# Third seven-product pair in the first two downs of each feed-forward, with the residual added in HBM

## The chip, the cores and the metric

One core of a Trainium2 chip (trn2) runs the whole block in one launch. The metric is device time in microseconds (us), the median of several executions. The engines are TensorE (PE; its weight loads are the separate row PEld), VectorE (DVE), ScalarE (ACT), GpSimd (POOL) and SyncE (SP), which here only issues DMA transfers.

## The reference

One layer of a streaming encoder on 256 tokens with 2048 features, in float32. Only the two feed-forwards matter here, each with 5632 hidden features:

```python
def swiglu(h, w_gate, w_up, w_down):
    return (jax.nn.silu(h @ w_gate) * (h @ w_up)) @ w_down

x = x + 0.5 * swiglu(rms_norm(x, ffn1_norm[l]), ...)
# pooling and gated linear attention on rms_norm(x), one output projection, added to x
# attention over 256 memory tokens, added to x
x = x + 0.5 * swiglu(rms_norm(x, ffn2_norm[l]), ...)
out = rms_norm(x)
```

## The kernel before

**Precision.** Every float32 operand is split into a high and a low part in fp32r: ScalarE copies the high part (`wh` of a weight, lines 279, 491, 1720), VectorE subtracts it to get the low part (`wl`, lines 280, 455). A product is then three matmuls: high by high, high by low, low by high.

**Units.** A projection is cut into units of one 1 MB weight load: two blocks of 128 rows (a pair) by 1024 columns. A plain unit multiplies both token halves by all four 128x512 blocks with 24 matmuls of 512 columns (`products`, line 362). A seven treats the pair as a 2x2 block matrix and takes 7 block products P1 to P7 in place of 8, 21 matmuls (`seven`, line 509). For that VectorE makes four sums of weight blocks (`T`, line 488), of which high and low parts are taken as well (`th`, `tl`; the plain blocks' parts are `rh`, `rl`, in the tiles xh and xl), and once per pair four sums of the activations (`Sums.make`, lines 426 to 438), whose parts go to the tile ye and back into ys. P1 and P2 need neither sum; P3 and P4 use a sum on one side alone: P3 one of activations, P4 one of weights. P5, P6 and P7 need both.

**A block** (`block_s`) is 8 units over 1024 columns. It accumulates in four PSUM tiles of two banks: two hold the directly usable results (P2 and P4; P3 and P0), two the partial ones (P1 and P6; P7 and P5). Only four such tiles exist. After the block's last seven, `combine` (lines 583 to 588: one ScalarE copy of P1, three VectorE sums) turns the partial ones into an SBUF tile `sg` and frees their PSUM tiles. After the block's last unit the two others are joined with it (`join`, line 598) or, if `merge` is given, the combined part has already been added to the residual (`early_parts`, line 781) and the rest is added straight from PSUM (`residual`, line 769).

**A feed-forward** (`ffn`) runs in three parts of 4, 4 and 3 column blocks of 512 hidden features. Each part has gate and up blocks (all of them with four sevens, `ORDER`), the turning of the hidden features into `ys` (transposes on line 791), and a down: two blocks of 1024 output columns, which the prediction calls the halves A and B. The first two downs of a part of four (`WHOLE`) have 8 units per half, two of them sevens (pairs 0 and 4). The residual lies in HBM, in X[0] and X[1]; in each half of a down it is fetched (`fetch_x`), added to, and stored again (`store_x`). The first down fetches the input instead.

**Order.** A `Stream` lists units and other steps; `st.op(f, n)` puts a step behind the next n units. Weights are split two units ahead (AHEAD) and loaded three (RAW). The low and high parts of weights form one chain on VectorE and one on ScalarE (`in_turn`); `among_weights` puts a step into that chain, so that it comes after the parts emitted so far and before the next ones. Buffers tie the two ends: wh and wl have three buffers each, so a unit's parts wait until the unit three places before it has left TensorE. A step marked as a `clump` tells the unit before it to hand the last 768 of its 2048 low-part columns to GpSimd (`low_parts`, line 459). Within these bounds the order on each engine is fixed when the kernel is built. All loads and stores of X and all weight loads are issued by SP, one after another.

Of the kernel before, what the change touches and what calls it, by code (L numbers as in the profile page):

```python
# [8 lines left out]
F32R = mybir.dt.float32r  # L9
AF = mybir.ActivationFunctionType  # L10
ALU = mybir.AluOpType
# [3 lines left out]
P = 128  # L15
D = 2048
S = 256
# [3 lines left out]
NB = 512  # L21
# [9 lines left out]
G_FFN1, G_MIX, G_X, G_MEM, G_FFN2, G_PS, G_HN, G_BA, G_END = 0, 16, 32, 48, 64, 80, 88, 96, 100  # L31
# [68 lines left out]
def build(ctx, tc, I, out):  # L100
    nc = tc.nc
    st = Stream()
# [7 lines left out]
    scope = {"stack": None}  # L110
# [34 lines left out]
    def uid(s):  # L145
        cnt[0] += 1
        return f"{s}{cnt[0]}"
# [21 lines left out]
    def ctl(name, shape):  # L169
        return whole_lines(const, shape, F32, name, name)  # L170
# [7 lines left out]
    for t in range(PAD):  # L178
        nc.gpsimd.memset(invc[:, t : t + 1], 1.0 / (t + 1))
    gains = ctl("gains", [P, G_END])  # L180
    Rcol = ctl("Rcol", [P, 2])
    Rm = ctl("Rm", [P, 2])
    ss = ctl("ss", [P, 2, 8])
    sums = ctl("sums", [P, 2])
# [85 lines left out]
    def among_weights(f):  # L270


        scalar, vector = behind_weights(f)
        latest["vector"] = vector
        if scalar is not None:
            latest["scalar"] = scalar
# [22 lines left out]
    def finish_norm(n, spread_too=True):  # L299

        nc.vector.tensor_reduce(out=sums, in_=ss[:, :, :n], axis=AX.X, op=ALU.add)
        done = rsqrt(Rcol, sums, D, 2)
        if spread_too:
            diag["R"] = [diagonal(Rcol[:, t : t + 1]) for t in range(2)]
        return done
# [100 lines left out]
    class Sums:  # L406
# [8 lines left out]
        def make(self, g):  # L415
            act, i = self.act, self.pairs.index(g)
            n = 3 if self.over else 4
            if self.own and (i == 0 or i >= self.room):
                room, tag = (self.room, self.name) if i == 0 else (1, f"{self.name}{i}")
                t = scope["pool"].tile([P, room * 6 * P], F32R, tag=tag, name=uid(tag))  # L420
                held = min(len(self.pairs), self.room) if i == 0 else 1
                t = t[:, : held * 2 * n * P].rearrange("p (g a n s) -> p g a n s", a=2, n=n, s=P)
                self.where.update({i + k: t[:, k] for k in range(held)})
            own = self.where[i]
            a, k = jtile(), slice(2 * g, 2 * g + 2)
            nc.vector.tensor_tensor(
                out=a.rearrange("p (k s) -> p k s", k=2), in0=f32(act[:, k, 0, :]),
                in1=f32(act[:, k, 1, :]), op=ALU.add,
            )

            a = a.rearrange("p (n s) -> p n s", n=4)
            p11, p21, p12, p22 = (a[:, m] for m in range(4))
            nc.vector.tensor_tensor(out=p11, in0=p11, in1=p21, op=ALU.subtract)
            nc.vector.tensor_tensor(out=p21, in0=p22, in1=p21, op=ALU.subtract)
            nc.vector.scalar_tensor_tensor(
                out=p22, in0=p11, scalar=-1.0, in1=p22, op0=ALU.mult, op1=ALU.subtract
            )
            added = nc.vector.tensor_tensor(out=p12, in0=p12, in1=p22, op=ALU.add)
            split(own[:, 0], own[:, 1], a[:, 4 - n :])
            if self.over:  # L440
                split(act[:, 2 * g, 0, P:], act[:, 2 * g, 1, P:], p11)
            return None, added
# [370 lines left out]
    class IntoX:  # L813
# [7 lines left out]
        def make_sums(self, after=None):  # L821
            for g, n in zip(self.sums.pairs, after or self.after):
                st.op(lambda g=g: among_weights(lambda: self.sums.make(g)), n)

    WHOLE = IntoX((0, 4), (2, 5), ((1, 2, 3, 5, 0, 6, 4, 7), (1, 2, 0, 3, 4, 5, 6, 7)),
                  ((0, 4), (0, 4)))
    MIXED = IntoX((0, 4), (1, 4), ((1, 2, 3, 6, 0, 5, 4, 7), (1, 2, 3, 0, 4, 5, 6, 7)),
                  ((0, 4), (0, 4)), room=2, folds=(1, 1, 2, 2))
    OUTPUT = IntoX((0, 4, 6), (0, 4, 9), ((1, 2, 3, 5, 0, 6, 4, 7), (1, 2, 0, 3, 4, 5, 6, 7)),
# [4 lines left out]
    def into_x(w, act, scale, gain=None, k0=0, nk=KT, spread_too=True, src=None, way=OUTPUT,  # L834
               spread_at=3, behind=None):

        for b in range(2):
            st.op(lambda b=b: fetch_x(b, src), 2)
            cols = wwide(w, b * 2 * NB, k0, nk)
            if way.sevens[b]:  # L840
                block_s(cols, act, way.sums, way.orders[b], residual(scale, b, 0),
                        early_parts(scale, b), way.sevens[b], behind=None if b else behind)
            else:
                block_t(cols, act, residual(scale, b))
            if gain is not None:
                for j in range(2):
                    st.op(lambda c=2 * b + j: fold(c, gain), way.folds[2 * b + j])
        if gain is not None:
            st.op(lambda: finish_norm(4, spread_too), way.folds[3] + 1)
            if spread_too:  # L850
                st.op(spread_norm, spread_at)

    FF_PARTS = ((0, 4), (4, 4), (8, 3))

# [4 lines left out]
    def ffn(wg, wu, wd, down, amid=None, end=None):  # L859
# [19 lines left out]
        def ev_up(j, c, held=gate):  # L879
            g = held[j]  # L880
            for h in range(2):
                nc.vector.scalar_tensor_tensor(
                    out=g[:, h, :], in0=c[:, h, :], scalar=Rcol[:, h : h + 1], in1=g[:, h, :],
                    op0=ALU.mult, op1=ALU.mult,
                )

# [53 lines left out]
        return nc.scalar.activation(sums, Rcol, AF.Silu), done  # L940

    st.op(lambda: among_weights(first_factor), 6)
    st.op(more_gains, 14)
    st.op(lambda: turn_gains(G_MIX, G_END), 35)

# [5 lines left out]

    def down_first(wd, k0, nk, last, way):
        way.make_sums()
        if last:
            for g, after in zip(qk_sums.pairs[:2], (9, 11)):
                st.op(lambda g=g: among_weights(lambda: qk_sums.make(g)), after)
        into_x(wd, ys, 0.5, G_MIX if last else None, k0, nk, src=None if k0 else I["x"][0],
               way=way, spread_at=7)

    ffn(I["ffn1_w_gate"][0], I["ffn1_w_up"][0], I["ffn1_w_down"][0], down_first,  # L960
        amid_first)
# [309 lines left out]
    def low_rank():  # L1271
# [4 lines left out]
            sevens=(1, 3))  # L1276
# [226 lines left out]
    def down_last(wd, k0, nk, last, way):  # L1503
        if last:
            down_end(wd, k0, nk, way)
        else:
            way.make_sums()
            into_x(wd, ys, 0.5, None, k0, nk, way=way)

    def end_parts(b):  # L1510
        def home():
# [7 lines left out]
    def down_end(wd, k0, nk, way):  # L1519
# [29 lines left out]
        def last_part(i):  # L1549
            return acc_ps[i][:, 0, : NB // 2]  # L1550
# [14 lines left out]
        def update(nb, h):  # L1565
            xn = x_cols(nb * NB, NB)[:, h]
            return nc.vector.scalar_tensor_tensor(
                out=xn, in0=acc_ps[nb][:, h, :], scalar=0.5, in1=xn, op0=ALU.mult, op1=ALU.add
            )

        def square(nb, h):
# [4 lines left out]
        def last_update(i):  # L1576
            xn = x_cols(3 * NB, NB)[:, 1, columns(i)]
            return nc.vector.scalar_tensor_tensor(
                out=xn, in0=last_part(i), scalar=0.5, in1=xn, op0=ALU.mult, op1=ALU.add
            )  # L1580

        def last_square(i):
# [96 lines left out]
        for b in range(2):  # L1679
            into = lambda j, ps: acc_ps.__setitem__(2 + j, ps)  # L1680
            block_s(wwide(wd, b * 2 * NB, k0, nk - 2), ys, way.sums, END_ORDER[b],
                    into if b else residual(0.5, 0, None), early_parts(0.5, b), (0,),
                    home=end_parts(b), more=b == 1)
        for b in range(2):
            st.unit(wwide(wd, b * 2 * NB, k0 + nk - 2, 2)[0], end_unit(b))
# [76 lines left out]
```

## Time and profile before

| what | value |
|---|---|
| median of 3 runs (lowest to highest) | 2071.29 us (2071.0 to 2071.98) |
| span of the profiled execution, first to last instruction | 2069.6 us |
| TensorE busy, instructions | 2059.1 us (99%), 9464 |
| VectorE busy | 1843.7 us (89%) |
| ScalarE busy | 1173.7 us (57%) |
| GpSimd busy | 103.5 us (5%) |
| mean granted TensorE clock | 0.999 of full |
| DMA: read and written in HBM | 417.58 MB, 16.78 MB |

The profiled execution has no time of its own beside its span: the median of the runs, which are timed without the profiler, is 1.7 us above the span. Matmuls are pipelined, one is issued every 0.227 us though each lasts 0.39 us, so busy times of single groups on TensorE overlap and the share of busy time says little; whether it waited is read from its waits. In a row of the profile stand the line, the engine, the operation, what is written <- what is read, the shape and the count; in the groups by line then the busy time, the mean length of one in ns, and the idle time of the engine before them with what ended it. In rows of the timeline, start and length in us come first. In rows of the stages the columns are the stretch and its length, then busy time of PE, PEld, DVE, ACT and POOL with instruction counts, the granted clock, the share and the rate of the DMA engines.

### The profile page before, as it was taken

Reading aid. Unit: us, or ns where it says so; the run is one execution under the profiler, and the core shown is the slowest. Engines: PE = TensorE matmul, PEld = TensorE weight load, DVE = VectorE, ACT = ScalarE, POOL = GpSimd, SP = SyncE. Lnnn points to the kernel's source line nnn. Section 1 sums busy time; section 2 is a strip of 40 time slices with the busy share of each in tenths; the row PEclk is TensorE's granted clock in tenths of the full one; section 3 lists DMA queues with packets and bytes.
Section 4 is the critical chain, followed back from the end, with each engine's and each line's share of the span. In section 5 each row is a group of like instructions: output and inputs, shape, how many; then the busy total and the mean of one; then the engine's idle time right before and its main releaser. Section 6 shows DMA issues by size and latency. Waiting matters only on the chain.

```text
span 2069.6 us, 24068 instructions
## 1 busy us (share of the span) xinstructions
PE 2059.1 (99%) x9464; PEld 1714.5 (83%) x9464; DVE 1843.7 (89%) x1720; ACT 1173.7 (57%) x1196; POOL 103.5 (5%) x93
## 2 busy tenths in 40 slices
PE   9999999999999999999999999999999999999998
PEld 7888888888888888888888888888888888888886
DVE  7998899989998779989889787989988999889987
ACT  7654455554554666665765544656554565545554
POOL 0000000000000000000000000000000010000001
PEclk9999999999999999999999999999999999999999
DMA  7666766566666655467655455666577765676664
GB/s 265 205 202 224 243 214 215 184 227 238 225 202 224 226 184 183 163 205 280 225 185 192 159 178 183 203 224 224 171 235 225 239 208 185 225 241 224 210 224 156
DMA packets 123129, 435.92 MB, mean 211 GB/s; under 512 B 9860, under 2 KB 13544, under 8 KB 122632
## 3 DMA queue, kind: packets, MB, share of 16 engines
q1 hardware_dynamic: 122840, 434.12, 62.9%
q8 instruction: 74, 1.21, 0.2%
q14 instruction: 39, 0.32, 0.0%
q10 hardware_dynamic: 176, 0.27, 0.0%
HBM read 417.58 MB, written 16.78 MB: 210 GB/s over the span
## 4 chain that ended last, share of the span: by engine, by line
PE 99%; DMA 0%; DVE 0%; SPq 0%; ACT 0%; POOL 0%; POOLq 0%; issue 0%; DVEq 0%
PE pt L362 64%; PE pt L509 30%; PE ph L791 2%; PE pl L1416 1%; PE pv L1453 1%; PE px L802 1%; PE pp L1049 0%; DMA x<-in_x 0%; PE pa L1077 0%; PE tm L1362 0%; PE po L1215 0%; PE px L728 0%; PE pq L1202 0%; PE pe L362 0%; PE pz L1093 0%; PE po L1218 0%
## 5 line engine op out<-in xcount | busy, mean ns | idle before, releaser
L362 PE MATMUL pt<-wh,xs 128*128 128x512 f32 x2432 | 780.8, 391 | 0.0
L1720 ACT CAST wh<-raw 128x2048 fp32r<-128x2048 f32 x242 | 461.7, 1912 | 228.9 <-PE pt L362 128.0
L455 DVE TENSOR_TENSOR wl<-raw,wh 128x2048 fp32r<-128x2048 f32 (+1 forms) x242 | 515.9, 2140 | 83.9 <-ACT wh L1720 83.7
L362 PEld LDWEIGHTS pt<-wh,xs 128*128 128x128 f32 x2432 | 455.9, 188 | 94.1 <-issue 0.5
L491 ACT CAST wh<-T 128x1024 fp32r<-128x1024 f32 x264 | 277.0, 1054 | 379.0 <-DVE T L488 362.4
L362 PE MATMUL pt<-wl,xs 128*128 128x512 f32 x1216 | 474.0, 390 | 0.0
L362 PE MATMUL pt<-wh,ys 128*128 128x512 f32 x1452 | 458.1, 389 | 0.0
L362 PEld LDWEIGHTS pt<-wh,ys 128*128 128x128 f32 x1452 | 272.5, 188 | 56.1
L455 DVE TENSOR_TENSOR wl<-T,wh 128x2048 fp32r<-128x2048 f32 (+1 forms) x132 | 296.7, 2248 | 5.6 <-ACT wh L491 5.2
L362 PE MATMUL pt<-wl,ys 128*128 128x512 f32 x726 | 283.0, 390 | 0.0
L362 PEld LDWEIGHTS pt<-wl,xs 128*128 128x128 f32 x1216 | 228.4, 188 | 46.2
L280 DVE TENSOR_TENSOR xl<-raw,xh 128x1536 fp32r<-128x1536 f32 x132 | 231.1, 1751 | 10.8 <-ACT xh L279 10.7
L279 ACT CAST xh<-raw 128x1536 fp32r<-128x1536 f32 x132 | 195.5, 1481 | 52.1 <-PE pt L509 30.7
L488 DVE TENSOR_TENSOR T<-T,raw 128x512 f32<-128x512 f32 x264 | 182.0, 690 | 6.8
L488 DVE TENSOR_TENSOR T<-raw 128x1024 f32<-128x1024 f32 x132 | 160.7, 1218 | 0.6
L362 PEld LDWEIGHTS pt<-wl,ys 128*128 128x128 f32 x726 | 136.3, 188 | 28.1
L509 PE MATMUL pt<-xh,xs 128*128 128x512 f32 x416 | 154.9, 389 | 0.0
L509 PE MATMUL pt<-wh,xs 128*128 128x512 f32 x396 | 153.9, 389 | 0.0
L459 POOL TENSOR_TENSOR wl<-raw,wh 128x768 fp32r<-128x768 f32 x44 | 81.6, 1854 | 1389.6 <-DVE wl L455 1366.8
L509 PE MATMUL pt<-wh,xe 128*128 128x512 f32 x320 | 124.3, 389 | 0.0
L509 PEld LDWEIGHTS pt<-xh,xs 128*128 128x128 f32 x416 | 78.1, 188 | 16.2
L509 PEld LDWEIGHTS pt<-wh,xs 128*128 128x128 f32 x396 | 74.3, 188 | 15.4
(274 smaller groups left out, 2081.4 us busy)
## 6 DMA issues: line engine op xcount, KB each, us to landing
raw<-in_ffn_w_down SPq DMA_DIRECT2D x88, 1024.0 KB, 5.5
raw<-in_ffn_w_up SPq DMA_DIRECT2D x80, 1024.0 KB, 5.0
raw<-in_ffn_w_gate SPq DMA_DIRECT2D x77, 1024.0 KB, 5.1
raw<-in_w_in SPq DMA_DIRECT2D x32, 1024.0 KB, 5.0
raw<-in_xattn_w_kv SPq DMA_DIRECT2D x32, 1024.0 KB, 5.0
raw<-in_w_out SPq DMA_DIRECT2D x16, 1024.0 KB, 6.7
raw<-in_xattn_w_q SPq DMA_DIRECT2D x16, 1024.0 KB, 6.2
raw<-in_xattn_w_o SPq DMA_DIRECT2D x16, 1024.0 KB, 5.7
```

Source lines behind the costliest of these rows:

```text
L279: in_turn("scalar", lambda: nc.scalar.copy(hi, src))
L280: in_turn("vector", lambda: nc.vector.tensor_tensor(out=lo, in0=src, in1=f32(hi), op=ALU.subtract))
L362: latest["product"] = nc.tensor.matmul(ps, a, w, start=first and i == 0, stop=last and i == 2)
L455: in_turn("vector", lambda: nc.vector.tensor_tensor(out=lo[:, :n], in0=src[:, :n], in1=f32(hi[:, :n]), op=ALU.subtract))
L459: rest = nc.gpsimd.tensor_tensor(out=lo[:, n:], in0=src[:, n:], in1=f32(hi[:, n:]), op=ALU.subtract)
L488: in_turn("vector", lambda: nc.vector.tensor_tensor(out=o, in0=a, in1=b, op=ALU.add))
L491: in_turn("scalar", lambda: nc.scalar.copy(th[:, c], t[:, c]))
L509: nc.tensor.matmul(banks[n], x, w, start=n in fresh and j == 0, stop=n in ends and j == 2)
L791: rows["turned"] = nc.tensor.transpose(v[:, i, h * P : (h + 1) * P], g[:, h, i * P : (i + 1) * P], ident)
L802: nc.tensor.transpose(v[:, j, h * P : (h + 1) * P], x[:, h, j * P : (j + 1) * P], ident)
L1416: nc.tensor.matmul(ps[:, t, :M], ys[:, 4 * h + d, a, tok], xa["K", h][:, d, b, :], start=i == 0, stop=i == 11,)
L1720: in_turn("scalar", lambda: nc.scalar.copy(hi, raw))
```

## The change

In the first two downs of both feed-forwards the residual no longer passes through SBUF. Each block joins its results in the tile `sg`, and a DMA issued by GpSimd adds that tile to X in HBM (`accum_op=ALU.add`), one transfer of 512 KB per 512 columns. For that X must hold the input from the start: SP copies the input to X inside HBM in 8 transfers of 256 KB, between the 15th and 29th unit of the first feed-forward. The factor 0.5 of the feed-forward moves to the up projection's row factor (`Rup`, one VectorE instruction per norm), and the last downs use 1.0. In the downs that now add in HBM, pair 2 becomes a third seven in each half, the order of the units changes, and the third pair's sums get a tile of the tag `sg`. Combine and joins stand in the chain of weight parts and are clumps there, as in gate and up blocks.

```diff
-    Rcol = ctl("Rcol", [P, 2])
+    factors = ctl("Rcol", [P, 4])
+    Rcol, Rup = factors[:, :2], factors[:, 2:]
...
-        done = rsqrt(Rcol, sums, D, 2)
+        rsqrt(Rcol, sums, D, 2)
+        done = nc.vector.tensor_scalar_mul(Rup, Rcol, 0.5)
...
-                room, tag = (self.room, self.name) if i == 0 else (1, f"{self.name}{i}")
-                t = scope["pool"].tile([P, room * 6 * P], F32R, tag=tag, name=uid(tag))
+                if i == 0:
+                    t = scope["pool"].tile([P, self.room * 6 * P], F32R, tag=self.name, name=uid(self.name))
+                else:
+                    t = scope["pool"].tile([P, 4 * NB], F32R, tag="sg", name=uid("sx"), bufs=2)
...
-    WHOLE = IntoX((0, 4), (2, 5), ((1, 2, 3, 5, 0, 6, 4, 7), (1, 2, 0, 3, 4, 5, 6, 7)),
-                  ((0, 4), (0, 4)))
+    WHOLE = IntoX((0, 4, 2), (2, 5, 4), ((1, 3, 5, 0, 6, 2, 4, 7), (1, 0, 3, 2, 5, 4, 6, 7)),
+                  ((0, 2, 4), (0, 2, 4)))
...
+    def copy_x(i):
+
+        b, rows_i = i % 2, slice(i // 2 * S // 4, (i // 2 + 1) * S // 4)
+        nc.sync.dma_start(X[b][rows_i, :], I["x"][0][rows_i, b * 2 * NB : (b + 1) * 2 * NB])
+
+    def added_to_x(b):
+
+        def evict(j, e):
+            nc.gpsimd.dma_start(
+                X[b][:, j * NB : (j + 1) * NB].rearrange("(h p) n -> p h n", p=P), e,
+                accum_op=ALU.add,
+            )
+        return evict
+
+    def onto_x(w, act, k0, nk, way):
+
+        for b in range(2):
+            block_s(wwide(w, b * 2 * NB, k0, nk), act, way.sums, way.orders[b], added_to_x(b),
+                    sevens=way.sevens[b])
...
-                    out=g[:, h, :], in0=c[:, h, :], scalar=Rcol[:, h : h + 1], in1=g[:, h, :],
+                    out=g[:, h, :], in0=c[:, h, :], scalar=Rup[:, h : h + 1], in1=g[:, h, :],
...
+    for i in range(8):
+        st.op(lambda i=i: copy_x(i), 15 + 2 * i)
...
     def down_first(wd, k0, nk, last, way):
         way.make_sums()
-        if last:
-            for g, after in zip(qk_sums.pairs[:2], (9, 11)):
-                st.op(lambda g=g: among_weights(lambda: qk_sums.make(g)), after)
-        into_x(wd, ys, 0.5, G_MIX if last else None, k0, nk, src=None if k0 else I["x"][0],
-               way=way, spread_at=7)
+        if not last:
+            onto_x(wd, ys, k0, nk, way)
+            return
+        for g, after in zip(qk_sums.pairs[:2], (9, 11)):
+            st.op(lambda g=g: among_weights(lambda: qk_sums.make(g)), after)
+        into_x(wd, ys, 1.0, G_MIX, k0, nk, way=way, spread_at=7)
...
-            into_x(wd, ys, 0.5, None, k0, nk, way=way)
+            onto_x(wd, ys, k0, nk, way)
```

The remaining lines put 1.0 for 0.5 where the last down of the second feed-forward is added (`update`, `last_update`, `residual`, `early_parts`).

More of the change, by code (lines that the diff above doesn't have):

```diff
@@ L1567, in update @@
             return nc.vector.scalar_tensor_tensor(
-                out=xn, in0=acc_ps[nb][:, h, :], scalar=0.5, in1=xn, op0=ALU.mult, op1=ALU.add
+                out=xn, in0=acc_ps[nb][:, h, :], scalar=1.0, in1=xn, op0=ALU.mult, op1=ALU.add
             )
@@ L1578, in last_update @@
             return nc.vector.scalar_tensor_tensor(
-                out=xn, in0=last_part(i), scalar=0.5, in1=xn, op0=ALU.mult, op1=ALU.add
+                out=xn, in0=last_part(i), scalar=1.0, in1=xn, op0=ALU.mult, op1=ALU.add
             )
@@ L1681, in down_end @@
             block_s(wwide(wd, b * 2 * NB, k0, nk - 2), ys, way.sums, END_ORDER[b],
-                    into if b else residual(0.5, 0, None), early_parts(0.5, b), (0,),
+                    into if b else residual(1.0, 0, None), early_parts(1.0, b), (0,),
                     home=end_parts(b), more=b == 1)
```

## The prediction

> **What bounds the kernel now.** I read the page first, then TensorE's own waits, then the first down stage engine by engine.
>
> ```profile
> span 2069.6 us, 24068 instructions
> PE 2059.1 (99%) x9464; PEld 1714.5 (83%) x9464; DVE 1843.7 (89%) x1720; ACT 1173.7 (57%) x1196; POOL 103.5 (5%) x93
> ```
> ```profile
> PE pwarm L206 <- POOL ident masks.py:199: 1.4, 1, 1.4
> PE px L728 <- DMA x<-in_x: 0.5, 1, 0.5
> ```
>
> The last two lines are the whole answer on TensorE's waits, and both are at the start. From then on it issues one product after another; VectorE at 89% is the next tightest. So a product removed is worth its full issue time, and that holds only until VectorE is late for the first time. Next, the turning of ys, a seven and a plain unit on PE (chain of the first down: start, length, products), and the first down's two column halves, A and B, in the stage table:
>
> ```profile
> 185.99 1.75 PE ph L791 x16
> ...
> 201.94 4.76 PE pt L509 x21
> 206.70 5.44 PE pt L362 x24
> ```
> ```profile
> 178.00:224.00 46.00, 46.00 (x214) 38.27 (x213) 39.04 (x41) 23.90 (x20) 0.24 (x1) 1.00 0.58 206
> 224.00:265.00 41.00, 41.00 (x182) 33.96 (x181) 39.74 (x31) 20.41 (x15) 0.00 (x0) 1.00 0.76 256
> ```
>
> 5.44/24 = 0.227 us per product, 4.76 us per seven. Columns three to five of the stage rows are PE, weight load and VectorE: VectorE works 39.0 of 46 us in A and 39.7 of 41 in B (the granted clock is 1.00). The question is whether the VectorE work of another seven fits, and at the right moment.
>
> **The change part by part.**
>
> *Products.* 4 downs x 2 halves x 1 more seven x 3 products x 0.227 us = 5.44 us less PE work (1.36 per down). That is all there is to win: 0.26%.
>
> *What VectorE loses and gains.* Rows of A's first down, from the VectorE timeline (start, length):
>
> ```profile
> 171.73 1.23 DVE L585 TENSOR_TENSOR sg<-pt,sg 128x1024 f32<-128x1024 f32 x1
> ...
> 182.10 2.28 DVE L455 TENSOR_TENSOR wl<-raw,wh 128x2048 fp32r<-128x2048 f32 x1
> 185.74 2.29 DVE L455 TENSOR_TENSOR wl<-raw,wh 128x2048 fp32r<-128x2048 f32 x1 [1.35 <-ACT wh L1720]
> ...
> 201.10 1.22 DVE L488 TENSOR_TENSOR T<-raw 128x1024 f32<-128x1024 f32 x1
> ...
> 205.36 2.28 DVE L455 TENSOR_TENSOR wl<-T,wh 128x2048 fp32r<-128x2048 f32 x1
> 207.56 0.68 DVE L426 TENSOR_TENSOR j<-ys 128x512 f32<-128x512 f32 x1
> ...
> 209.47 0.29 DVE L438 TENSOR_TENSOR j<-j 128x128 f32<-128x128 f32 x1
> 209.68 2.28 DVE L455 TENSOR_TENSOR wl<-raw,wh 128x2048 fp32r<-128x2048 f32 x1
> 211.88 0.55 DVE L286 TENSOR_TENSOR ye<-j,ye 128x384 fp32r<-128x384 f32 x1
> ...
> 219.60 0.69 DVE L584 TENSOR_TENSOR sg<-pt,sg 128x512 f32<-128x512 f32 x1 [3.14 <-ACT sg L583]
> ```
>
> and, from the groups by line (count, busy, mean ns of one, idle time before):
>
> ```profile
> L781 DVE SCALAR_TENSOR_TENSOR x<-sg,x 128x1024 f32<-128x1024 f32 x26 | 31.4, 1216 | 0.0
> ...
> L583 ACT COPY sg<-pt 128x512 f32<-128x512 f32 x39 | 22.8, 586 | 57.8 <-PE pt L509 56.7 <-issue 1.1
> ...
> L459 POOL TENSOR_TENSOR wl<-T,wh 128x768 fp32r<-128x768 f32 x6 | 11.2, 1863 | 393.8 <-DVE wl L455 393.8
> ```
>
> Costs go from start to start, since instructions overlap a little: a plain unit's low part 2.2 (209.68 to 211.88), a seven 6.46 (201.10 to 207.56; its low part alone 2.2), the sums of ys for one pair 2.1 (207.56 to 209.68) plus about 0.5 for the low part of ye, and anything of 128x1024, as L781, a join or the low part of a turned block, 1.15 (its 1.22 less the same overlap). Per half the change adds 6.46 - 2.2 = 4.3 for the seven and half a set of sums, 1.3. It removes two of L781, 2.3 (L769 turns into a join of the same size), and, because combine and joins now stand as clumps, two low parts hand 768 of 2048 columns to GpSimd (L459, 1.86 there), 768/2048 of 2.2, 0.8 each: 1.6. Net +1.7 per half, while PE's time falls by 0.7. On average that still fits A; what matters is when it comes.
>
> *The order in A, step by step.* Let T=0 be the down's first product (178.12). The new order is plain 1, plain 3, plain 5, seven 0, plain 6, seven 2, seven 4, plain 7; the three sums are due after units 2, 4 and 5. VectorE is through with unit three's low part at 184.3, T=6.2, as now, and from there its order is forced:
> seven 0 +6.46 = 12.7; turned low parts 2.3 and sums 0 2.1: 17.1; plain 6: 19.3; seven 2: 25.8; sums 2, 2.6: 28.4; seven 4: 34.8; sums 4: 36.9 (their high part, a ScalarE copy under L583's 0.59, by 37.4); plain 7's low part: 39.1; low part of sums 4: 39.6.
> The same list for the kernel before (plain 5, sums 0, turns, seven 0, plain 6, seven 4) ends seven 4 at 207.56, T=29.4: its present 1.35 us of idle time goes, and 6.9 us are added (4.3 + 2.6).
> PE needs: four plain units 21.8, two sevens 9.5 and 16 transposes 1.8 take it to T=33.1. Of seven 4, three products (P1, P2, P4: 9 matmuls, 2.0 us) need no sums, but P4 needs the low part of 34.8, so PE is done with them at about 35.2. Then it can issue plain 7's first product in each of its four banks (0.9) and P7's two high ones (0.45), and waits for the high part of the sums at 37.4: 0.9 idle. Six products follow to 38.8, then it waits again for 39.1 to 39.6: 0.3 to 0.8. That is 1.2 to 1.7 with full filling. What it can't avoid even if every filler is placed well: 0.9. If nothing is filled in, it stands from 35.2 to 39.1: 3.9. TensorE's order is fixed when the kernel is built. Today's shows filling, not always the best:
>
> ```profile
> 214.18 0.23 PE pt L362
> 214.40 1.36 PE pt L509 x6
> 215.76 2.49 PE pt L362 x11
> 218.26 1.36 PE pt L509 x6
> ```
>
> In the same chain, where seven 4 ends today, products of the last plain unit (L362) stand among the seven's (L509). So I take 1.8 per down, nearer the filled end. Below zero it cannot go: there is no TensorE wait left to recover.
>
> *The next places.* After A, low part of B's first unit 1.4 (T=41.0), combine after seven 4's last product (about 40.9, then ScalarE's 0.6 and 0.69 + 1.2 + 0.69): 44.1; B's second unit is now seven 0, 5.6 with its shared low part: 49.7; the two joins 2.3: 52.0. PE gets to that seven at 43.3 + 1.8 + 5.4 = 50.5, and 9 of its products go into banks that the joins don't hold: 52.5. It fits by 0.5. Behind it the sevens of B alternate with plain units (4.76 + 5.44 on PE against 6.46 + 2.2), and VectorE regains its lead. B thus keeps its 0.68.
>
> *Transfers.*
>
> ```profile
> X<-x SPq DMA_DIRECT2D x28, 512.0 KB, 6.9
> x<-X SPq DMA_DIRECT2D x28, 512.0 KB, 4.2
> ...
> x<-in_x SPq DMA_DIRECT2D x8, 256.0 KB, 7.7
> ```
> ```profile
> ACT wh L1720 <- DMA raw<-in_ffn_w_down: 11.3, 7, 2.9
> ```
>
> SP loses 16 stores and 16 fetches. A store waits on SP for the residual, and weight loads queue behind it: ScalarE's 11.3 us of waiting for down weights. TensorE waited for none of it: worth nothing. SP gains 8 copies of 256 KB inside HBM, ahead of weight loads in the first feed-forward; the nearest row lands in 7.7 us, the weights are asked for three units (15 us) ahead: nothing, or if uncovered one late load of the present size, 2.9 us at most. The 16 adding transfers have no row. By the nearest (6.9 us for 512 KB) and even at five times that, 35 us, the next writer of their tile is the combine of the next gate block, seven units (some 36 us) on, and the next reader of X is a whole feed-forward part away. They stand behind VectorE's joins on GpSimd's queue, where the next instruction is a shared low part some 20 us later. Nothing, then; 0 to 2 us if the queue costs something at the start or end. The extra two-column multiplication at four norms is under the 0.29 us of a 128x128 sum (L438) each, and no PE wait stands there now: nothing, 1.2 at most.
>
> *Sum.* 4 x (1.8 - 1.36) = +1.8 us on the span of 2069.6; the median of the runs, 2071.29, lies 1.7 above that span and I keep that distance: 2073.1. Unknown ends per down: 0.9 and 3.9 idle give -1.8 and +10.2 us in all.
>
> **The rivals.**
>
> *Faster: the third seven is absorbed.* If PE's fixed order fills the hole or VectorE gets there 1.5 us earlier than I count, idle time is at most 0.3 per down: 2071.3 - 4.2 = 2067.1, at best 2065.9. For it: no PE wait at all today, and that seven 4's low part today comes 4.3 us before its unit starts (T=29.4 against 33.8, which is five plain units, a seven and the transposes). Against it: its low part comes 5.4 us later, and PE needs it 0.7 earlier.
>
> *Slower: B's second unit waits for A's joins.* Today combine starts at T=41.5, since 11 products of the plain unit are issued ahead of the seven's last six. If that is kept behind plain 7's low part, they end at 39.1 + 17 x 0.227 = 43.0, combine at 46.2, the joins at 54.1, 1.6 after the 52.5 where PE runs out: 1.8 + 1.6 idle per down, 4 x (3.4 - 1.36) = +8.2: 2079.5. It decides from seven 4's last product later than T=41.4 on (40.9 and the 0.5 to spare).
>
> *Slower: GpSimd's pieces hold VectorE up.* The change adds four pieces of a low part per down.
>
> ```profile
> 171.23 1.86 POOL L459 TENSOR_TENSOR wl<-raw,wh 128x768 fp32r<-128x768 f32 x1 [44.03 <-DVE wl L455]
> ```
>
> The combine's sum that starts within this one, at 171.73, reads PSUM and takes 1.23, as long as one of its size with no piece beside it (201.10: 1.22). If a piece came to lie beside a seven's sums and those had to wait for it, one per down at B's second unit would cost 1.86 - 0.5 = 1.4: 4 x 1.4 on top of the forecast, 2078.7. Against it: the pieces stay tied to units ahead of combine and joins. [...]
>
> **How the numbers follow.** This kernel's measurement can tell about 0.2% (4.1 us) from no change. Forecast (0.9 to 2.3 idle per down: -1.8 to +3.8) 0.46, with its own range 2069.5 to 2075.1; absorbed 0.22; joins late (or nothing filled in at A's pair of sevens, the 3.9) 0.27; pieces in the way 0.05. So faster 0.22, same 0.46, slower 0.32. The range reaches from the middle of the absorbed case, 2067, to the slower one's, 2080.
>
> **What the profile after would show.** Products: 9440 instead of 9464 on PE. L781 at 10 instead of 26, 16 more GpSimd-issued transfers, X<-x at 12 on SP. Right: in each first-half A a PE gap of 1 to 2 us at the second of two sevens in a row, VectorE without idle time for the 33 us before, and B without a gap. Wrong if PE shows no such gap (then VectorE's chain is shorter than 39 us or PE had more to fill in), if the gaps are at B's second unit, or if TensorE waits for weights or for X.

## The result: 2099.69 us, slower by 1.35%

| kernel | median of its runs | ratio to before, 95% interval |
|---|---|---|
| before | 2071.49 us | 1 |
| after | 2099.69 us (2095.7 to 2103.02) | 1.0135 [1.0123, 1.0147] |

The profiled execution took 2103.02 us (span 2101.2); it is the longest of the four runs. Every number of the trace of after is to be held against that span: +31.6 us on the span of before. The page of after, span and busy times:

```profile
span 2101.2 us, 24114 instructions
...
PE 2069.2 (98%) x9440; PEld 1713.6 (82%) x9440; DVE 1860.3 (89%) x1768; ACT 1188.6 (57%) x1220; POOL 150.9 (7%) x124
```

The products went as planned (9440 instructions), VectorE has only 17 us more to do in all, and yet TensorE's busy time rose by 10 us with fewer products in it. Its waits (releaser, us in total, times, longest):

```profile
PE pt L513 <- ACT ye L286: 11.3, 4, 3.5
PE pt L513 <- ACT xh L280: 2.6, 2, 1.5
PE pt L513 <- DVE wl L459: 2.5, 4, 0.6
PE pt L364 <- DVE wl L459: 1.6, 1, 1.6
...
PE pt L513 <- DVE sg L602: 1.2, 4, 0.3
PE pt L513 <- ACT ys L286: 1.2, 4, 0.3
```

Lines are shifted by a few (362 is 364, 509 is 513, 455 is 459, 285/286 is 286/287). The first line is new and the largest: in each of the four downs one seven stands for 2.4 to 3.5 us, and not for VectorE but for ScalarE, which makes the high part of the sums (`ye`). The fourth line is a single wait at the start. The first down, timeline of ScalarE, then SyncE's queue, TensorE and VectorE (start, length; in brackets the idle time before and what ended it):

```profile
216.12 3.70 ACT L1747 CAST wh<-raw 128x2048 fp32r<-128x2048 f32 x2
219.96 0.30 ACT L286 CAST ys<-j 128x128 fp32r<-128x128 f32 x1
221.76 1.47 ACT L280 CAST xh<-raw 128x1536 fp32r<-128x1536 f32 x1 [1.50 <-DMA raw<-in_ffn_w_down]
223.14 0.51 ACT L286 CAST ye<-j 128x384 fp32r<-128x384 f32 x1
...
216.86 6.88 SPq L642 DMA_DIRECT2D raw<-in_ffn_w_down  x2
...
219.06 0.50 PE L513 MATMUL pt<-wl,ys 128*128 128x512 f32 x1 [0.63 <-DVE wl L459]
...
220.31 0.50 PE L513 MATMUL pt<-wh,ys 128*128 128x512 f32 x1 [0.29 <-ACT ys L286]
...
223.70 0.80 PE L513 MATMUL pt<-xh,ye 128*128 128x512 f32 x1 [2.42 <-ACT ye L286]
224.29 0.63 PE L513 MATMUL pt<-xl,ye 128*128 128x512 f32 x1
...
215.04 1.75 DVE L281 TENSOR_TENSOR xl<-raw,xh 128x1536 fp32r<-128x1536 f32 x1
216.71 2.29 DVE L459 TENSOR_TENSOR wl<-T,wh 128x2048 fp32r<-128x2048 f32 x1
218.92 0.68 DVE L430 TENSOR_TENSOR j<-ys 128x512 f32<-128x512 f32 x1
...
220.82 0.29 DVE L442 TENSOR_TENSOR j<-j 128x128 f32<-128x128 f32 x1
```

Read it backwards. TensorE stands until 223.70 for `ye`. ScalarE began that copy at 223.14, although VectorE had had the sums ready at 221.11 (last of L442). In between ScalarE copied `xh`, the direct blocks of a seven's weights, and before that it had stood idle for 1.50 us for their transfer. That seven is B's second unit. Its transfer was issued at 216.86, just after VectorE's L281 of seven 4 had ended (216.79) and given the raw buffer back.

The second thing in those rows is the length of the matmuls after the wait: 0.63 and 0.43 from one start to the next, where 0.39 and 0.227 were usual. Stages around that wait and around the one at the start (columns as in the stage rows of before; the column after the five engines is the granted clock):

```profile
220.30:223.70 3.40, 0.97 (x3) 0.49 (x4) 3.37 (x5) 1.88 (x2) 0.00 (x0) 0.97 0.24 98
223.70:227.10 3.40, 3.40 (x8) 2.74 (x9) 1.49 (x2) 0.00 (x0) 2.02 (x1) 0.52 0.77 240
227.10:230.50 3.40, 3.40 (x16) 2.81 (x15) 0.00 (x0) 0.44 (x1) 0.00 (x0) 1.00 0.90 296
...
35.80:39.20 3.40, 3.40 (x10) 2.63 (x9) 2.75 (x5) 2.63 (x4) 0.00 (x0) 0.50 1.02 418
```

After the wait TensorE was granted half its clock for 3.4 us: 8 matmuls where 3.4/0.227 = 15 fit. There are five such stretches (at 35.8, 223.5, 479.5, 1592.3 and, twice as long, 1848.3), 20.4 us together. For 2.3 us of them TensorE was still waiting, and each matmul in the rest takes 0.427 in place of 0.227 us; counted so, the half clock cost 8.5 us, 7.1 of it in the downs. These stretches are "busy" time in the page, which is the largest part of why TensorE's busy time rose. The kernel before has none until its last matmul.

Where the 31.6 us went, counted on TensorE as start-to-start time above 0.227 us, in the steps longer than 0.33 us: 30.5 in the four downs (6.3, 6.2, 9.0 and 9.0), 4.6 more than before in the first 50 us (1.5 of it the clock), -5.4 for the products; about 2 us are spread over the rest and not assigned. The 30.5 are 18.8 us of waits, 7.1 of half clock and 4.6 that the steps beside the waits take longer.

### The profile page after: what moved, and what is told of

The parts are those of the page before. It is cut to its first block, busy times and chain, and to the rows that moved or that the text cites. A ratio compares the mean times of both kernels' runs of the same rounds, so it can differ in the third digit from the quotient of the medians.

```text
span 2101.2 us, 24114 instructions
## 1 busy us (share of the span) xinstructions
PE 2069.2 (98%) x9440; PEld 1713.6 (82%) x9440; DVE 1860.3 (89%) x1768; ACT 1188.6 (57%) x1220; POOL 150.9 (7%) x124
## 4 chain that ended last, share of the span: by engine, by line
PE 92%; DVE 3%; DMA 3%; ACT 1%; issue 0%; SPq 0%; POOL 0%; POOLq 0%; DVEq 0%; ACTq 0%
PE pt L364 57%; PE pt L513 30%; DMA raw<-in_ffn_w_down 2%; PE ph L795 1%; DVE T L492 1%; DMA raw<-in_ffn_w_gate 1%; ACT xh L280 1%; DVE wl L459 1%; PE pl L1443 1%; PE pv L1480 1%; DVE xl L281 1%; PE px L806 0%; DMA x<-in_x 0%; DVE sg L602 0%; PE pp L1076 0%
## 5 line engine op out<-in xcount | busy, mean ns | idle before, releaser
L1747 ACT CAST wh<-raw 128x2048 fp32r<-128x2048 f32 x234 | 445.8, 1912 | 199.8 <-PE pt L364 104.5
L459 DVE TENSOR_TENSOR wl<-raw,wh 128x2048 fp32r<-128x2048 f32 (+1 forms) x234 | 487.8, 2095 | 71.5 <-ACT wh L1747 71.3
L495 ACT CAST wh<-T 128x1024 fp32r<-128x1024 f32 x280 | 294.0, 1054 | 384.3 <-DVE T L492 373.5
L364 PE MATMUL pt<-wh,ys 128*128 128x512 f32 x1324 | 422.2, 391 | 0.0
L459 DVE TENSOR_TENSOR wl<-T,wh 128x2048 fp32r<-128x2048 f32 (+1 forms) x140 | 312.7, 2233 | 6.9 <-ACT wh L495 6.5
L364 PEld LDWEIGHTS pt<-wh,ys 128*128 128x128 f32 x1324 | 249.9, 189 | 51.9
L364 PE MATMUL pt<-wl,ys 128*128 128x512 f32 x662 | 259.5, 392 | 0.0
L280 ACT CAST xh<-raw 128x1536 fp32r<-128x1536 f32 x140 | 207.3, 1480 | 88.3 <-PE pt L513 39.5
L281 DVE TENSOR_TENSOR xl<-raw,xh 128x1536 fp32r<-128x1536 f32 x140 | 245.2, 1751 | 10.8 <-ACT xh L280 10.7
L463 POOL TENSOR_TENSOR wl<-raw,wh 128x768 fp32r<-128x768 f32 x56 | 104.4, 1864 | 1410.8 <-DVE wl L459 1388.0
```

The lines of the kernel that those rows point to most:

```text
L280: in_turn("scalar", lambda: nc.scalar.copy(hi, src))
L281: in_turn("vector", lambda: nc.vector.tensor_tensor(out=lo, in0=src, in1=f32(hi), op=ALU.subtract))
L364: latest["product"] = nc.tensor.matmul(ps, a, w, start=first and i == 0, stop=last and i == 2)
L459: in_turn("vector", lambda: nc.vector.tensor_tensor(out=lo[:, :n], in0=src[:, :n], in1=f32(hi[:, :n]), op=ALU.subtract))
L463: rest = nc.gpsimd.tensor_tensor(out=lo[:, n:], in0=src[:, n:], in1=f32(hi[:, n:]), op=ALU.subtract)
L495: in_turn("scalar", lambda: nc.scalar.copy(th[:, c], t[:, c]))
```

## The experiments

All are set against the kernel before, which ran beside them on the same chips (its medians 2071.47 to 2071.71 us). "Held" means that the copies of the input to X are tied to the weight load before them.

| experiment | median, us | ratio, 95% interval |
|---|---|---|
| e1, copies held | 2098.81 | 1.0133 [1.0116, 1.015] |
| e11, the kernel before with the copies alone | 2074.49 | 1.0013 [1.0004, 1.0022] |
| e7, two sevens, held | 2072.92 | 1.0007 [0.9998, 1.0017] |
| e3, ScalarE's copy of the sums first | 2092.0 | 1.0097 [1.0082, 1.0112] |
| e6, sevens of A spread, held | 2101.25 | 1.0143 [1.0128, 1.0158] |
| e9, third seven in A alone, held | 2080.18 | 1.0038 [1.0025, 1.0052] |
| e8, third seven in B alone, held | 2075.32 | 1.0015 [1.0007, 1.0024] |
| e10, pieces to GpSimd around the sums, held | 2091.13 | 1.009 [1.0076, 1.0104] |
| e12, both, B's second unit plain, held | 2077.21 | 1.0028 [1.0016, 1.004] |
| e13, third seven in B alone, second unit plain, held | 2070.29 | 0.9993 [0.9984, 1.0002] |

**The copies: e1 and e11.** In after, the eight copies were not spread over units 15 to 29: SyncE issued them all between 21.3 and 28.2 us, amid the first weight loads.

```profile
21.27 1.24 SPq L860 DMA_DIRECT2D X<-in_x  x2
22.61 0.53 SPq L642 DMA_DIRECT2D raw<-in_ffn_w_gate  x1
23.18 3.12 SPq L860 DMA_DIRECT2D X<-in_x  x4
26.40 0.54 SPq L642 DMA_DIRECT2D raw<-in_ffn_w_gate  x1
26.98 1.19 SPq L860 DMA_DIRECT2D X<-in_x  x2
...
30.40 1.91 ACT L1747 CAST wh<-raw 128x2048 fp32r<-128x2048 f32 x1 [3.03 <-DMA raw<-in_ffn_w_gate]
```

ScalarE stood 3.0 us for its weights, VectorE 4.4 us for ScalarE's high part, TensorE 1.6 us for the low part (fourth line of the waits). e1 holds the copies:

```diff
-        nc.sync.dma_start(
+        latest["load"] = nc.sync.dma_start(
...
-        nc.sync.dma_start(X[b][rows_i, :], I["x"][0][rows_i, b * 2 * NB : (b + 1) * 2 * NB])
+        with tc.issue_after(latest["load"].ins):
+            nc.sync.dma_start(X[b][rows_i, :], I["x"][0][rows_i, b * 2 * NB : (b + 1) * 2 * NB])
```

> The changed kernel with one edit: each of the 8 copies of the input to X is queued on SP behind the latest weight load, so none can be issued in the first 30 us. Theory (copies drawn forward to 21 to 28 us delay two weight loads, TensorE waits 1.6 us and then runs 3.4 us at half clock): the 4.9 us lost in the first 50 us come back, 2099.7 becomes about 2095, the granted clock shows no half-rate stretch at 36 us, and the four downs are as they were. Rival (the start is lost to GpSimd's queue or to chance): 2099.7 and the gap at 33 us stays.

2098.81 us. In its profile the wait and the half clock at the start are gone, the downs are as in after (`ye` 10.7 us in 4 waits, clock halved behind them). The medians differ by only 0.9 us and their runs overlap (2097.99 to 2100.69 against 2095.7 to 2103.02), so the start's 4.6 us are seen in one profile and not in the times. What is sure is that the downs hold nearly all of the loss. e11 hoists only the copies into the kernel before:

```diff
+    def copy_x(i):
...
+    for i in range(8):
+        st.op(lambda i=i: copy_x(i), 15 + 2 * i)
```

> The kernel before with the 8 copies of the input to X added where the change has them, and nothing else; X is overwritten later as before, so they are idle transfers. Theory (drawn forward to some 21 to 28 us, they delay two weight loads): TensorE waits about 1.6 us near 32 us and the time rises by 1.5 to 5 us, 2073 to 2076.5, the more when the clock halves behind the wait. Rival (that wait came from elsewhere): 2071.5.

2074.49 us, +2.8 (interval 0.8 to 4.6). Its profile shows ScalarE's casts waiting up to 1.4 us for weights near 30 us, but no wait of TensorE there; what stands out on TensorE is a wait of 2.2 us for the input at the very start, with 3.4 us of half clock right behind it. That start wait varies from profile to profile (none in the waits of e7 and e10, 2.2 us here), so how the 2.8 us arise is not settled. That the copies, issued there, cost something is.

**The adds: e7.** Everything of the change but the third seven, with the old orders:

```diff
-    WHOLE = IntoX((0, 4, 2), (2, 5, 4), ((1, 3, 5, 0, 6, 2, 4, 7), (1, 0, 3, 2, 5, 4, 6, 7)),
-                  ((0, 2, 4), (0, 2, 4)))
+    WHOLE = IntoX((0, 4), (2, 5), ((1, 2, 3, 5, 0, 6, 4, 7), (1, 2, 0, 3, 4, 5, 6, 7)),
+                  ((0, 4), (0, 4)))
```

> The changed kernel with two edits: the copies held back as in the run with that edit alone, and the first two downs with two sevens per half in the order of before. What stays of the change: the sums added to X by GpSimd-issued transfers, joins and combine as clumps, the factor 0.5 in the up projection. Theory (the adding transfers cost nothing by themselves; all of the loss is the third seven and the copies): 2071.5, within 2 us of before, and no TensorE wait after the start. Rival (the adding transfers or their issue on GpSimd take from weight loads or from VectorE): 2076 or more, with TensorE waits in the downs or behind them.

2072.92 us, +1.4 with an interval that takes in zero. TensorE waits for nothing in the downs that use the adds. Sixteen GpSimd-issued transfers that add in HBM, clumps, row factor and held copies together cost 3.5 us at most, by the interval: nearly all of the loss comes with the third seven.

**Does moving ScalarE's copy cure it? e3.** The sums are made to return the high part's copy, so that ScalarE's later casts come behind it (in the first two downs of each feed-forward alone; copies not held):

```diff
-            split(own[:, 0], own[:, 1], a[:, 4 - n :])
+            high, _ = split(own[:, 0], own[:, 1], a[:, 4 - n :])
...
-            return None, added
+            return high if self.pairs == (0, 4, 2) and self.act is ys else None, added
```

> The changed kernel with one edit: in the downs that add in HBM, ScalarE's high part of the sums (ye, sx) is put into the chain of weight parts, so that the next weights' high parts come after it. Theory (TensorE waits at the pair of sevens because ScalarE stands before that cast, waiting for a weight load that VectorE's lateness delayed, and the long wait then halves the clock): the four waits for ye of 2.4 to 3.5 us become under 1 us, the low parts of the sums become the next wait, about 1 us, the half-clock stretches in the downs go, and the time falls by 8 to 14 us to 2086 to 2092. Rival (TensorE has to wait for VectorE's chain anyway, ScalarE's order only names the last of several late parts): the wait moves to the low part, the time falls by less than 3 us, and the clock still halves.

2092.0 us. The `ye` wait falls from 11.3 to 1.7 us, and others come, since all casts of weights are now behind the copy:

```profile
PE pt L364 <- DVE wl L459: 7.0, 5, 1.6
PE pt L513 <- DVE xl L281: 4.7, 4, 1.2
PE pt L513 <- DVE wl L459: 3.1, 4, 0.8
PE pt L513 <- ACT ys L286: 2.1, 4, 0.5
PE pt L513 <- ACT ye L286: 1.7, 4, 0.4
```

They add up to 17.0 us in the downs (1.6 of the first row is at the start), nearly as much as in after (18.8), but none is longer than 1.6 us, and nowhere in the profiled run is the clock halved before the last matmul (mean 0.999, after 0.994). Start to start the downs lose 22.5 us, 8.0 less than in after, about the clock's share there (7.1). So in the profiles part of the loss is the clock's. The medians don't price it: three other runs of e3 were granted 0.997, 0.997 and 0.998 and took no longer (2091.74, 2092.26 and 2090.68 against 2092.27).

Nor is it a cure to put ScalarE's copy ahead of all casts. VectorE's last sums now end 39.2 us from the first down's start, where in after they ended at 37.6, since the casts that its low parts need come later: VectorE began one at 200.61 behind 1.7 us of idle time that ScalarE's cast (L1747) ended. Plain 7's cast belongs before the copy, B's second unit behind it; that is the order of e9 and e12 below.

**Is it the pair of sevens at A's end? e6.** Held, copy first as in e3, and A ordered like B, so that no two sevens stand together:

```diff
+    WHOLE = IntoX((0, 4, 2), (0, 4, 2), ((1, 0, 3, 2, 5, 4, 6, 7), (1, 0, 3, 2, 5, 4, 6, 7)),
                  ((0, 2, 4), (0, 2, 4)))
```

> The changed kernel with three edits: copies held back, the sums' high part first on ScalarE, and in half A the order of half B, 1 0 3 2 5 4 6 7, in which the three sevens alternate with plain units (sums due after 0, 4 and 2 units). Theory (the loss in A is three sevens and two sets of sums in a row that VectorE cannot work off in time; alternating them leaves it 6.5 + 2.2 us of work for 10.2 us of products): TensorE waits under 0.5 us per down, no half clock, and the 5.4 us of products are won in part: 2066 to 2070. Rival (VectorE's work per down is too much in any order, or seven 0 in second place is late itself behind the up block): waits of 1 to 3 us per down move to the front of A, 2072 to 2085.

2101.25 us, the slowest of all, with the clock whole (0.999). The waits start right behind the turning of ys and run through A: low parts 7.1 us in 8, `ys` 6.4 in 4, `ys` from ScalarE 4.2 in 8. I read this as VectorE entering a down without a lead, so that the plain units belong at A's front, as the change has them; no run tests that by itself.

**Which half? e9 and e8.** e9 keeps A of the change and gives B its old order with two sevens; its pair 2 in B is a plain unit that multiplies activations which the sums have partly overwritten (same work, other values). e8 has A as before and the three sevens in B, with pair 2's sums due within B. The lines of the change, then those of e9, then those of e8:

```diff
-    WHOLE = IntoX((0, 4, 2), (2, 5, 4), ((1, 3, 5, 0, 6, 2, 4, 7), (1, 0, 3, 2, 5, 4, 6, 7)),
-                  ((0, 2, 4), (0, 2, 4)))
...
+    WHOLE = IntoX((0, 4, 2), (2, 5, 4), ((1, 3, 5, 0, 6, 2, 4, 7), (1, 2, 0, 3, 4, 5, 6, 7)),
+                  ((0, 2, 4), (0, 4)))
...
+    WHOLE = IntoX((0, 4, 2), (2, 5, 9), ((1, 2, 3, 5, 0, 6, 4, 7), (1, 0, 3, 2, 5, 4, 6, 7)),
+                  ((0, 4), (0, 2, 4)))
```

> The changed kernel with the copies held back and the third seven in half A alone: A as in the change, B with the order and the two sevens of before. 12 products less than before, 2.7 us. Theory (A carries the loss): the waits for the sums' high parts stay at 2.3 to 3.5 us per down with half-clock stretches behind them, 2094 to 2099, near the change with held copies (2098.8). Rival (A and B share it: B's late joins and ScalarE's early place for B's second unit, a seven whose weights land late, make A's wait): with a plain unit in B's second place ScalarE has no seven's copy ahead of the sums' part, the waits shrink to the VectorE chain's 1 to 2 us without half clock, 2076 to 2084.

> The changed kernel with the copies held back and the third seven in half B alone: half A has the order and the two sevens of before, half B those of the change, the sums of pair 2 are due after 9 units, in B. 12 products less than before, 2.7 us. Theory (the loss in the downs comes from A's chain; B with its alternating sevens has room): no TensorE wait over 0.3 us in the downs, 2072.9 (two sevens in both halves) less 2.7 is 2070.2, under before by about 1.3. Rival (a third seven is too much for VectorE in either half, or seven 0 in B's second place waits for the joins): waits of 0.5 to 2 us per down at B's second or sixth unit, 2073 to 2080.

e9: 2080.18 us. A is the same as in after, and yet its `ye` wait is 0.4 us per down, not 2.8:

```profile
PE pt L513 <- DVE wl L459: 2.8, 5, 0.6
PE pt L513 <- ACT ye L286: 1.7, 4, 0.4
...
PE pt L513 <- ACT ys L286: 1.2, 4, 0.3
```

So how long A waits is decided by what stands in B. e8: 2075.32 us, 2.4 above e7 with 2.7 us of products less; TensorE waits 1.8 us (4 times 0.5) for `xl` of B's second unit, and its profile has a wait of 1.8 us for the input at the start. Over e7 the third seven costs 7.3 us in A alone and 2.4 in B alone, 9.7 together; e1, with both, costs 25.9. The two halves disturb each other, and what e9 lacks of e1 is a third seven in B with a seven in B's second place.

**GpSimd beside the sums: e10.** The sums of the first two downs are clumps too, so that the units ahead of them hand 768 columns of low parts to GpSimd:

```diff
-                st.op(lambda g=g: among_weights(lambda: self.sums.make(g)), n)
+                f = lambda g=g: among_weights(lambda: self.sums.make(g))
+                st.op(clump(f) if self is WHOLE else f, n)
```

> The changed kernel with the copies held back and the three sums per down marked as clumps, so that GpSimd takes 768 of 2048 low-part columns of the three units ahead of them in A. Theory by VectorE's work (2.4 us less of it ahead of the pair of sevens): the wait at the sums falls by 1 to 2.4 us per down, and with it the half clock: 2082 to 2092. [...]

2091.13 us, 7.7 below e1, but not because VectorE has the sums sooner. Seven 4's low part comes 0.6 us earlier (34.8 from the first down's start at 178.32, after 35.4), yet the sums behind it end later, at 38.3 where after has 37.6; in the three other downs it is the same. They meet GpSimd's piece (GpSimd, VectorE, ScalarE, first down):

```profile
213.36 2.12 POOL L463 TENSOR_TENSOR wl<-T,wh 128x768 fp32r<-128x768 f32 x1 [7.49 <-DVE wl L459]
...
213.13 0.69 DVE L430 TENSOR_TENSOR j<-ys 128x512 f32<-128x512 f32 x1
213.86 1.77 DVE L437 TENSOR_TENSOR j<-j 128x128 f32<-128x128 f32 x1
215.67 0.29 DVE L438 TENSOR_TENSOR j<-j 128x128 f32<-128x128 f32 x1
...
216.32 0.29 DVE L442 TENSOR_TENSOR j<-j 128x128 f32<-128x128 f32 x1
...
216.65 0.52 ACT L286 CAST ye<-j 128x384 fp32r<-128x384 f32 x1 [0.68 <-DVE j L442]
217.06 1.48 ACT L280 CAST xh<-raw 128x1536 fp32r<-128x1536 f32 x1
```

L437 and L438 are of one shape. The one that comes while the piece runs takes 1.77 us, ending with it, the next 0.29. This is what the third rival supposed, at 1.5 us a meeting (1.77 less 0.29); the rival priced a meeting at the whole piece, 1.86, of which 0.5 was to spare. At the two other pieces beside sums in this down, at 191.53 and 203.72, L437 takes 0.82 and 1.82 us, and ends within 0.2 us of the piece. What is won goes with ScalarE's order, in all four downs: `ye` is now copied as soon as its sums are there, and `xh` comes behind it. Why the order turned here was not followed up. TensorE still waits 10.9 us for `ys` in 4 waits, up to 2.7, and the clock is halved three times.

**B's second unit plain: e12 and e13.** e12 is e1 with one tuple changed, e13 is e8 with the same:

```diff
-    WHOLE = IntoX((0, 4, 2), (2, 5, 4), ((1, 3, 5, 0, 6, 2, 4, 7), (1, 0, 3, 2, 5, 4, 6, 7)),
+    WHOLE = IntoX((0, 4, 2), (2, 5, 4), ((1, 3, 5, 0, 6, 2, 4, 7), (1, 3, 0, 5, 2, 6, 4, 7)),
                   ((0, 2, 4), (0, 2, 4)))
```

> Held copies, three sevens in both halves, A as in the change; only B's order differs: 1 3 0 5 2 6 4 7, so that its second unit is a plain one and not seven 0. Theory (a seven in B's second place puts ScalarE's copy with its late weights in front of the sums' high part): A's waits fall to those with the third seven in A alone, 1.36 us per down (2.46 counted from matmul start to start), no stretch at half clock, none at B's joins; 2072.9 (two sevens, held) + 4 x 2.46 - 2.7 (three more products... in each B, 4 x 0.68) - 2.7 (in each A) + up to 1.6 for the start = 2077 to 2079. Rival (it is the sum of VectorE's work in A and B that is too much, wherever it stands): single waits over 2 us remain or come back in B, half clock with them, 2088 to 2099.

> Held copies, third seven in B alone, B's order 1 3 0 5 2 6 4 7 in place of 1 0 3 2 5 4 6 7. Theory: the waits of B's second unit (1.8 us by the waits, 0.86 per down from start to start) go, since a plain unit of 5.4 us now stands ahead of the first seven: 2075.3 - 3.4 = 2071.9, level with the kernel before. Rival: VectorE is short of time in B as a whole and the wait moves to a later seven, 2075 to 2077.

e12: 2077.21 us, 21.6 below e1 with the same sevens, sums, copies and adds. TensorE's waits in the downs are those of e9, row for row: 2.8 us for low parts, 1.7 for `ye`, 1.2 for `ys`. Against e1's profile 9.0 us of waits for `ye` are gone (10.7 to 1.7), 3.3 of waits in B (`xh` 2.1, L602 1.2) and 7.4 of half clock. ScalarE and TensorE at the same place:

```profile
216.36 0.51 ACT L286 CAST ye<-j 128x384 fp32r<-128x384 f32 x1 [0.88 <-DVE j L442]
...
222.59 1.91 ACT L1748 CAST wh<-raw 128x2048 fp32r<-128x2048 f32 x1
...
216.11 0.40 PE L513 MATMUL pt<-wh,ys 128*128 128x512 f32 x1
216.92 0.50 PE L513 MATMUL pt<-xh,ye 128*128 128x512 f32 x1 [0.42 <-ACT ye L286]
217.26 0.39 PE L513 MATMUL pt<-xl,ye 128*128 128x512 f32 x1
217.49 0.40 PE L513 MATMUL pt<-wh,ye 128*128 128x512 f32 x1
```

This down starts at 178.72 and that of after at 183.49. VectorE's sums end at 37.6 us from the down's start in both. ScalarE copies them at once here (end 38.2) and after `xh` there (end 40.2); the cast of B's second unit, now a plain one, comes 5.7 us after the copy. No clock is halved before the last matmul, and B waits for nothing. The sum closes: e7's 2072.9, less 5.4 for products, plus 4 x 2.45 us lost start to start per down (counted as for after), is 2077.3.

That ScalarE's order is what changed can be seen in the rows. Why a plain unit's cast keeps out of the way and a seven's copy doesn't is not tested by itself. The buffers allow a reading, not shown by a run: `wh` has three, so a plain unit's cast can't be set before the unit three places earlier has left TensorE, while `xh` has a buffer of its own and could be put ahead in ScalarE's order as soon as its weights were reckoned to be there.

e13: 2070.29 us; the `xl` waits of e8 are gone, and beside the waits at the very start one of 0.3 us is left. It is 2.6 below e7, its 2.7 us of products. Against before, 0.9993 [0.9984, 1.0002]: the best found, not clear of no change.

## Why the prediction was wrong

Forecast 2073.1 (2067 to 2080), measured 2099.69. By its steps:

- **Products, -5.44 us: right.** 9440 on TensorE; of e13's half of it, 2.7 us, the medians of e7 and e13 show 2.6.
- **VectorE's order in A: right within 0.7 us.** Seven 4's low part was forecast for T=34.8 and came at 35.4 (218.92 - 183.49); sums 4 at 36.9, came at 37.6.
- **"their high part, a ScalarE copy ..., by 37.4": the step that failed.** It came at 40.2 in the first down and at 40.0 to 41.1 in the others; where nothing stood in front of it (e9, e12) it came at 38.0 to 38.2. I followed VectorE's queue instruction by instruction and gave ScalarE's 0.5 us without asking what stands in front of it. B's second unit had just become a seven, I counted it on VectorE ("fits by 0.5") and on no other engine. Its copy stood ahead, waiting for weights.
- **"the weights are asked for three units (15 us) ahead: nothing": failed.** It was said of the copies, and late loads of the downs were not priced at all. A load starts when its raw buffer comes back, and a VectorE without idle time gives it back late: asked for at 216.86, there at 221.7, wanted by ScalarE from 220.3. The copies were taken to be spread over 15 units and were all issued by 28.2 us; the bound "one late load ... 2.9 us at most" was close to ScalarE's 3.03, but left out the clock. What TensorE lost by it is 4.6 us in the profile and not seen in the medians (e1).
- **PE idle 1.8 per down: the place was right, the size off, and where it fits that is partly luck.** The gap came at the second of two sevens, as forecast, but at 2.4 to 3.5 us where 1 to 2 was the sign of being right. With ScalarE on time, e9 and e12 wait 1.35 us per down, inside the 1.2 to 1.7 forecast; the parts differ, though. The forecast had next to nothing for seven 4's low part, 0.9 for the high part and 0.3 to 0.8 for the low part of the sums; measured are 0.63 for seven 4's low part, 0.72 for the high parts (`ys` 0.30, `ye` 0.42) and no listed wait for the low part. And a stop costs more than its wait: in e12's rows from 216.11 to 217.49 three steps take 1.38 us where 0.68 is usual, 0.70 lost for a wait of 0.42. Per down it is 2.45, not 1.8.
- **A halved clock behind a wait was no term at all.** It cost 8.5 us in after's profile. The upper end, "nothing is filled in ... 3.9", was a bound on idle time at full clock.
- **Adding transfers, nothing: right** as far as e7 can tell (+1.4 us, interval -0.4 to 3.5, with all that goes with them).
- **Rivals.** "Absorbed" is refuted in A. "B's second unit waits for A's joins" named the right unit and the wrong way: it does wait for the joins, 0.3 us each (L602), but its harm lay in ScalarE's order, one half earlier, where no rival looked. "Pieces hold VectorE up": no run or row had shown a sum that waits for a piece, so its 1.4 us per down was the author's estimate. e10 shows one of 1.77 us beside a piece where 0.29 is usual. It is not what happened in after, where each L437 in the downs that add takes 0.28 or 0.29.

## What to carry to other kernels

When a unit of work moves, walk every in-order engine that serves it, at its new place, and ask what then stands behind it: here the order of B's units, not the added work, made 21.6 us. Price a stall of the matmul engine at more than its wait (0.70 us lost for 0.42 waited), and look at the granted clock behind it. In these profiles single stops up to 1.6 us within the downs never cost the clock; of those of 2.3 us and more all but one did.

## What the hardware did that was not expected

- The clock was halved at waits of 2.2 to 3.5 us (after, e1, e10, and e11 at its start), in stretches of 3.4 or 6.8 us, once after 1.6 us at the start (after, 35.8), but not in e3 after the same 1.6, nor in the first down of e10 after 2.7; and not in e6, e9 or e12. Most of the waits that did it were shorter than the stretch that goes with them: in after 1.59, 2.42, 2.42 and 3.48 us with 3.41, and 2.99 with 6.83.
- What went with it can be read from the traces. In after the stretches start at 35.79, 223.52, 479.52, 1592.27 and 1848.27, all whole multiples of 3.413 us apart, and last that long or twice that. Counting on from such a start in steps of 3.413 us cuts a profile into cells. Here are the cells before two stretches of after and one of e10, then the two cells of e10's first down (behind a cell's length comes TensorE's busy time, as the profile models it):

```profile
32.38:35.79 3.41, 1.82 (x8) 1.19 (x8) 3.38 (x4) 2.35 (x10) 0.00 (x0) 1.00 1.03 418
220.11:223.52 3.41, 0.97 (x3) 0.49 (x3) 3.34 (x6) 1.91 (x3) 0.00 (x0) 1.00 0.29 119
467.13:470.54 3.41, 0.70 (x4) 0.27 (x2) 3.31 (x5) 2.42 (x3) 2.10 (x1) 1.00 0.92 303
...
211.13:214.54 3.41, 2.17 (x10) 1.34 (x8) 3.38 (x4) 3.41 (x3) 1.18 (x1) 1.00 0.45 112
214.54:217.95 3.41, 1.93 (x8) 1.50 (x9) 3.31 (x5) 1.90 (x4) 0.94 (x1) 1.00 0.48 196
```

  In after TensorE was busy for 1.82, 0.97, 1.17, 0.86 and 1.77 us in the cells before the five stretches, and for 1.78 in the first half of the double one; of the cells at full clock that none followed, the least busy have 1.83 (at 2090.61, with the last matmul in it) and 1.93 (at 1585.44). All 13 stretches of the twelve profiles that begin before the last matmul follow a cell in which TensorE was busy for 0.69 to 1.82 us. No cell at full clock with more than 1.83 us was followed by one. At 1.82 or 1.83 it went either way, and one cell with 1.60, at the end of e1, was not followed. In e10 waits of about 2.7 us went with a half clock in three downs and not in the first, where the border of two cells, at 214.54, cuts the wait and TensorE is busy for 2.17 and 1.93 us in them. Where the cells lie differs from profile to profile: counted from the first instruction, one begins at 35.79 in after and one at 2064.43 in before, 594.3 cells apart.
- Issuing two adding transfers of 512 KB took GpSimd 2.57 us (after, first down), where SyncE issued two copies of 256 KB in 1.24. TensorE waited for none of it in e7.

```profile
240.97 2.57 POOL L865 DMA_DIRECT2D X<-sg  x2
```
